# Stores taken one product later, ACT copies for the rotary swap, and token differences under the first head, in a diffusion layer kernel on one core

## The chip, the core and the metric

One program runs on one core of a Trainium2 chip. Five engines work side by side and wait for each other by semaphores: TensorE (PE in the profile, with its weight loads as PEld), VectorE (DVE), ScalarE (ACT), GpSimd (POOL) and SyncE (SP), whose queue here issues nearly all DMAs. Each engine takes its instructions strictly in the order in which the built program lists them, so an instruction that waits holds all that stand behind it. The metric is device microseconds for one execution.

## The reference

One layer over 1024 latent tokens and 256 context tokens, D = 1024, 4 retention heads and 4 mLSTM heads of width 128, then a SwiGLU feed-forward part of width 2816 and a last norm. Shortened:

```python
hx = modulate(rms_norm(x, norm1_gain), sh1, sc1)
rq, rk, rv, rg, mq, mk, mv, mo, mg, bg_ret, bg_ml = (hx @ w for w in split(w_in))
rq, rk = apply_rope(rq, cos, sin), apply_rope(rk, cos, sin)   # halves of each head: t1*cos - t2*sin, t2*cos + t1*sin
ret, ml = bidirectional_scans(...)                            # chunks of 128 tokens, both directions, context first
y_ret = head_norm(ret) * silu(rg)
y_ml = head_norm(sigmoid(mo) * ml)
merged = sigmoid(bg_ret) * (y_ret @ w_ret_up) + sigmoid(bg_ml) * (y_ml @ w_ml_up)
x = x + g1 * (merged @ w_out)
x = x + g2 * swiglu(modulate(rms_norm(x, norm2_gain), sh2, sc2), w_ffn_in, w_ffn_out)
return rms_norm(x, final_gain)
```

## The kernel before

**Products.** Activations stand with features on the partitions. Each float32 operand is split into a high and a low half (`split`: ACT makes the high half, DVE the low one), and a product is 12 matmuls of 128x128x512. The 16 input blocks of the 8 heads (for head `u`, part 0 is k and v, part 1 is q and the gate) and the 8 blocks of the branch gates `bg` are 256 output columns each. All but the first head's run as `winograd_block`: seven products in place of eight, over sums and differences of the four token quadrants (`t1` to `t4`, the token differences) and of the weight quadrants (`Factors`). Products 1, 3, 5 and 7 add up in one PSUM tile (`ch`), the others use two `ts` tiles; DVE or ACT takes the four results out (`put`, line 279) into `kt` tiles, and snapshots of the chain are ACT copies (line 284).

**The first head** is computed directly, since the differences aren't there yet: eight pieces of product for the first 512 tokens, four with `kh` 0 and four with `kh` 1 for the others, the gate product in between. Only then are the token differences built (lines 656 to 668): for each of four k tiles DVE and POOL form differences in `wt` tiles and `split` writes `t1` to `t4`.

**Side work.** `run_blocks` calls `tick` after each product. A tick does what `pending` holds (transposes of k and v to token layout, delayed by 2 or 4 ticks) and then advances generators: `gates` (the mLSTM gate rows, with running sums along 1280 tokens as DVE scans, lines 709 and 710), `scan(u)` (both directions of a head's scan: kv chunks loaded through a ring of six `kv` tiles, decayed on POOL at line 814, multiplied at line 828, added on DVE at line 833), and `ada2`. A scheduler turns the code into one list per engine, by its own guess of when each thing is ready.

**Rotary.** For retention heads `rotated` swaps the two partition halves of a result by two DMAs of 64x512 each (lines 562 and 563), POOL multiplies by sin (565), DVE by cos and adds (567, 568, or 570, 571 for q). The tables `cosT`, `sinT` are loaded once.

**Stores.** Each result is stored by a DMA that SP issues directly behind its producer in the code (lines 557, 579, 588, 590, 930, 991); SP waits in its queue until the result is there, and loads stand behind it.

**y_ret.** At the seventh `bg` block `load_y_ret` first drains all side work, then loads eight tiles of the retention output and splits them, all before that block's own work in the code; `load_split` and `Factors` share three `stg` tiles.

## Time and profile before

| | before |
|---|---|
| median of 3 runs | 1673.01 us (1670.24 to 1678.15) |
| the profiled execution | 1677.59 us, span 1675.8 us |
| PE busy | 1584.7 us, 95% of the span, 7478 matmuls |
| DVE, ACT, POOL busy | 1003.3 us (60%), 704.5 us (42%), 459.4 us (27%) |
| chain that ended last | PE 74%, DVE 8%, DMA 7%, POOL 4%, ACT 3% |
| DMA | 261.39 MB, mean 156 GB/s |

PE is the bound over the whole span, but the shares hide stages: from 1060 us on PE hardly pauses, and most of what it waits for lies in the first 770 us. So the stretches are read one by one, with what PE waited for in each.

### The profile page before, as it was taken

To read this page: it belongs to the slowest core of one execution; us is meant where nothing else is said; L and a number is where in the kernel's file an instruction comes from. 1 tells how busy PE (TensorE), PEld (TensorE's weight loads), DVE (VectorE), ACT (ScalarE), POOL (GpSimd) and SP (SyncE) were. 2 spreads that over 40 slices of the span, in tenths; PEclk is the share of its full clock that TensorE was granted. 3 is DMA by queue.
4 is the path that set the end of the run, shared out by engine and by line. 5 is a ranking of instruction groups with operands and counts; after the bars stand their busy time and mean duration, and the time that the engine had idled before them with its cause. 6 is when DMAs were issued, how large, how long until landed. Compare 5 with 4: busy or idle time off the path is not lost.

```text
span 1675.8 us, 22635 instructions
## 1 busy us (share of the span) xinstructions
PE 1584.7 (95%) x7478; PEld 1286.0 (77%) x7478; DVE 1003.3 (60%) x1835; ACT 704.5 (42%) x1370; POOL 459.4 (27%) x512
## 2 busy tenths in 40 slices
PE   7999889989999899988999999999999999999997
PEld 2677667777887778777888777888888888888887
DVE  4575896767667776655444667555555554636343
ACT  3653433444435466565223344344343334524230
POOL 0133424444344345420121225222222322001001
PEclk9999899999999999998999999999999999999998
DMA  8753337777668676544646332222222224835531
GB/s 286 261 157 112 92 92 236 225 221 229 216 205 254 209 217 199 183 134 155 200 145 218 114 95 83 82 89 82 95 82 88 84 81 145 272 105 169 182 96 51
DMA packets 186469, 261.39 MB, mean 156 GB/s; under 512 B 19264, under 2 KB 85952, under 8 KB 186352
## 3 DMA queue, kind: packets, MB, share of 16 engines
q1 hardware_dynamic: 184480, 257.85, 48.6%
q10 hardware_dynamic: 1872, 2.10, 0.4%
q8 instruction: 59, 0.97, 0.2%
q14 instruction: 58, 0.48, 0.1%
HBM read 199.30 MB, written 56.38 MB: 153 GB/s over the span
## 4 chain that ended last, share of the span: by engine, by line
PE 74%; DVE 8%; DMA 7%; POOL 4%; ACT 3%; issue 3%; SPq 1%; DVEq 0%; POOLq 0%; ACTq 0%
PE ch L249 22%; PE ts L249 18%; DMA kv<-kv_d 3%; PE ch L1257 2%; PE ch L1256 2%; PE ch L1255 2%; PE ts L1257 2%; PE ts L1255 2%; PE ts L1256 2%; PE sc L395 2%; DMA stg<-wada 1%; POOL hid L1125 1%; PE ts L104 1%; PE ch L104 1%; PE ts L103 1%
## 5 line engine op out<-in xcount | busy, mean ns | idle before, releaser
L183 DVE TENSOR_TENSOR fw<-raw,fw 128x512 fp32r<-128x512 f32 x305 | 225.8, 746 | 147.7 <-ACT fw L182 144.5
L249 PE MATMUL ts<-A,fw 128*128 128x512 f32 x1200 | 300.1, 397 | 2.1 <-DVE A L387 0.9
L182 ACT CAST fw<-raw 128x512 fp32r<-128x512 f32 x305 | 187.5, 620 | 257.7 <-PE ch L1257 84.5
L249 PE MATMUL ch<-A,fw 128*128 128x512 f32 x1176 | 291.6, 396 | 0.0
L249 PE MATMUL ch<-t,fw 128*128 128x512 f32 x1008 | 257.3, 401 | 6.7 <-ACT u L284 3.6
L249 PEld LDWEIGHTS ts<-A,fw 128*128 128x128 f32 x1200 | 224.6, 190 | 50.4 <-DVE A L387 3.0
L249 PEld LDWEIGHTS ch<-A,fw 128*128 128x128 f32 x1176 | 219.3, 189 | 46.4 <-issue 1.0
L249 PEld LDWEIGHTS ch<-t,fw 128*128 128x128 f32 x1008 | 189.1, 192 | 46.6 <-ACT u L284 4.2
L249 PE MATMUL ts<-t,fw 128*128 128x512 f32 x504 | 133.7, 410 | 24.6 <-ACT fw L182 8.4
L1125 POOL TENSOR_TENSOR hid<-hid,sg 128x512 f32<-128x512 f32 x44 | 90.2, 2062 | 214.7 <-DVE hid L279 198.1
L249 PEld LDWEIGHTS ts<-t,fw 128*128 128x128 f32 x504 | 96.5, 196 | 46.9 <-ACT fw L182 8.8
L221 POOL TENSOR_TENSOR stg<-raw,raw 128x512 f32<-128x512 f32 x42 | 62.7, 1494 | 225.9 <-DVE fw L183 95.1
L284 ACT COPY u<-ch 128x512 f32<-128x512 f32 x104 | 60.8, 585 | 142.0 <-PE ch L249 136.2
L183 DVE TENSOR_TENSOR fw<-stg,fw 128x512 fp32r<-128x512 f32 x126 | 97.2, 771 | 30.9 <-ACT fw L182 30.8
L182 ACT CAST fw<-stg 128x512 fp32r<-128x512 f32 x126 | 78.3, 623 | 70.8 <-DVE stg L221 41.0
L814 POOL TENSOR_SCALAR vs<-kv,dcol 128x128 f32<-128x128 f32 x72 | 57.8, 808 | 58.8 <-DMA kv<-kv_d 34.6
L1247 POOL TENSOR_SCALAR cp<-cp,cpack 128x256 f32<-128x256 f32 (+1 forms) x6 | 8.2, 1361 | 222.2 <-ACT stg L1301 222.2
L828 PE MATMUL sc<-vs,kv 128*128 128x128 f32 (+1 forms) x288 | 52.1, 284 | 16.1 <-POOL vs L814 12.4
L814 POOL TENSOR_SCALAR vs<-kv,colq 128x129 f32<-128x129 f32 x72 | 51.9, 726 | 45.7 <-DMA kv<-kv_d 21.9
L828 PEld LDWEIGHTS sc<-vs,kv 128*128 128x128 f32 x288 | 44.8, 192 | 23.8 <-POOL vs L814 14.9
L183 DVE TENSOR_TENSOR fw<-s,fw 128x512 fp32r<-128x512 f32 x42 | 30.7, 732 | 43.5 <-ACT fw L182 43.4
L959 DVE SCALAR_TENSOR_TENSOR acc<-stg,silu_c,acc 128x512 f32<-128x512 f32 x56 | 43.9, 784 | 17.6 <-DMA stg<-wada 17.1
(363 smaller groups left out, 2918.4 us busy)
## 6 DMA issues: line engine op xcount, KB each, us to landing
raw<-wffn SPq DMA_DIRECT2D x88, 256.0 KB
raw<-wfo SPq DMA_DIRECT2D x88, 256.0 KB
kv<-kv_d SPq DMA_DIRECT2D x152, 128.0 KB
raw<-win SPq DMA_DIRECT2D x64, 256.0 KB
stg<-wada SPq DMA_DIRECT2D x64, 256.0 KB
hid_d<-hid SPq DMA_DIRECT2D x44, 256.0 KB
hraw<-hid_d SPq DMA_DIRECT2D x40, 256.0 KB
araw<-wada SPq DMA_DIRECT2D x32, 256.0 KB
```

The lines of the kernel that those rows point to most:

```text
L182: nc.scalar.copy(hi, x)
L183: nc.vector.tensor_tensor(out=lo, in0=x, in1=hi.bitcast(F32), op=ALU.subtract)
L221: eng.tensor_tensor(out=o, in0=x, in1=y, op=op)
L249: nc.tensor.matmul(ps, lhsT=w[wp_][:, c], rhs=x[xp][k], start=start and k == i == 0, stop=cont or (stop and k == 3 and i == 2), skip_group ...
L284: nc.scalar.copy(o, chain)
L814: nc.gpsimd.tensor_scalar(out=vs, in0=kv[d, n][1], scalar1=col, scalar2=None, op0=ALU.mult)
L828: nc.tensor.matmul(ps, lhsT=kv[d, n][0], rhs=vsd.pop((d, n)), start=True, stop=True)
L959: nc.vector.scalar_tensor_tensor(out=acc, in0=raw, scalar=s, in1=acc, op0=ALU.mult, op1=ALU.add)
L1125: nc.gpsimd.tensor_tensor(out=c, in0=c, in1=sgs[f, hf], op=ALU.mult)
L1255: nc.tensor.matmul(ps, lhsT=w[0][:, c], rhs=h[0][:, t], start=kt == 0, stop=False)
L1256: nc.tensor.matmul(ps, lhsT=w[0][:, c], rhs=h[1][:, t], start=False, stop=False)
L1257: nc.tensor.matmul(ps, lhsT=w[1][:, c], rhs=h[0][:, t], start=False, stop=kt == 2 * NG - 1)
```

## The change

Six edits. (1) Every store, gate store and y store is put into `pending` by `later(1, store, ...)` or `later(2, ...)`, so that SP gets it one or two ticks after its producer. (2) `rotate` runs one tick after its result and swaps the halves by two ACT copies; it loads its 512 columns of cos and sin each time (256 KB each, from the ring of two `rp` tiles). (3) The token differences are built inside the first head: `first_factor` behind each of the four `kh` 0 pieces, `other_factors` behind the gate product. (4) Two 36x1280 subtractions of `gates` go from DVE to POOL. (5) The `kv` ring has 8 tiles, `wt` 5; y results use `wt` and the `bg` results `kt`. (6) `load_y_ret` is a generator beside the last two `bg` blocks, a tile per tick, loaded three ticks ahead of its split, through `wt`.

```diff
-        return pw.tile([P, 512], dt, tag="wt", bufs=4, name=nm("wt"))
+        return pw.tile([P, 512], dt, tag="wt", bufs=5, name=nm("wt"))
...
+    def store(dst, src):
+        nc.sync.dma_start(dst, src)
...
-        nc.sync.dma_start(dst, o.rearrange("p (n c) -> p n c", n=4))
+        later(1, store, dst, o.rearrange("p (n c) -> p n c", n=4))
+
+    def rotate(c, hf, scale):
+        cs, sn = (pw.tile([P, 512], F32, tag="rp", bufs=2, name=nm("rp")) for _ in range(2))
+        for t, key in ((cs, "cosT"), (sn, "sinT")):
+            nc.sync.dma_start(t, a[key][:, hf * 512:hf * 512 + 512])
+        sw = wt()
+        nc.scalar.copy(sw[0:64], c[64:P])
+        nc.scalar.copy(sw[64:P], c[0:64])
+        nc.gpsimd.tensor_tensor(out=sw, in0=sw, in1=sn, op=ALU.mult)
...
-            sw = wt()
-            nc.sync.dma_start(sw[0:64], c[64:P])
-            nc.sync.dma_start(sw[64:P], c[0:64])
...
+            if f == 0:
+                if ret:
+                    later(1, rotate, c, hf, QSCALE if part else None)
+                elif part:
+                    nc.scalar.activation(c, c, AF.Copy, scale=QSCALE)
+                later(2 if ret else 1, store, qk_d[u][:, 1 - part, t], c)
+                if part == 0:
+                    later(4 if ret else 2, transpose_out, c, kv_d[u][:, n0, 0, :])
...
-                if kh == 1:
+                if kh == 0:
+                    first_factor(2 * key + f)
+                else:
...
             gate_products(CTX + 512, 512, lambda i, kt: xh[1][i][:, kt, :])
+            for k in range(4):
+                other_factors(k)
...
-        nc.vector.tensor_tensor(out=gi, in0=gi, in1=bb, op=ALU.subtract)
-        nc.vector.tensor_tensor(out=bb, in0=bb, in1=m, op=ALU.subtract)
+        nc.gpsimd.tensor_tensor(out=gi, in0=gi, in1=bb, op=ALU.subtract)
+        nc.gpsimd.tensor_tensor(out=bb, in0=bb, in1=m, op=ALU.subtract)
...
-            t = bt([P, 2 * P + 1], "kv", 6)
+            t = bt([P, 2 * P + 1], "kv", 8)
...
-            nc.sync.dma_start(y_d[u, j0 // 4], sy)
+            later(1, store, y_d[u, j0 // 4], sy)
...
                 if blk == 6:
-                    load_y_ret()
+                    drain()
+                    es_b.close()
+                    beside(load_y_ret())
...
+        raws_ = []
+        for i in range(11):
+            if i < 8:
+                raws_.append(wt())
+                nc.sync.dma_start(raws_[i], y_d[i % 4, i // 4])
+            if i >= 3:
+                hf, k = (i - 3) // 4, (i - 3) % 4
                 y_ret[hf].append(tuple(py_.tile([P, 512], F32R, name=nm("yr")) for _ in range(2)))
-                load_split(y_d[k, hf], *y_ret[hf][k])
+                split(*y_ret[hf][k], raws_[i - 3])
+            yield
```

The matmuls of PE are the same in number and kind. What moves is the order on the engines that feed it, at three places.

ACT, end of the first head, before: `e` is the gate product's result, `kt` the first head's four results for the second 512 tokens (line 641), `fw` weight halves, `t` and `A` the halves of the token differences (`wt` their inputs).

```order
L615 COPY e_1305<-sc_1288 128x512
L641 COPY kt_1320<-ts_1228 128x512
L182 CAST fw_1505<-stg_1503 128x512
L641 COPY kt_1341<-ch_1249 128x512
L182 CAST fw_1533<-stg_1531 128x512
L641 COPY kt_1355<-ts_1262 128x512
L182 CAST fw_1536<-raw_1483 128x512
L641 COPY kt_1384<-ch_1275 128x512
L556 COPY wt_1381<-sc_1376 128x512
L182 CAST t_1390<-wt_1388 128x512
```

The same place of the change (the `kt` copies are line 668 now; lines 564 and 565 are the new swap copies):

```order
L616 COPY e_1333<-sc_1316 128x512
L182 CAST t_1373<-wt_1369 128x512
L182 CAST A_118<-wt_1370 128x512
L182 CAST t_1394<-wt_1384 128x512
L668 COPY kt_1412<-ts_1229 128x512
L182 CAST fw_1514<-stg_1512 128x512
L182 CAST t_1389<-wt_1385 128x512
L182 CAST A_118<-wt_1386 128x512
L564 COPY wt_1430<-kt_1412 64x512
L565 COPY wt_1430<-kt_1412 64x512
L668 COPY kt_1436<-ch_1258 128x512
```

Before, no half of a token difference stood ahead of the four `kt` copies; now the halves of the third and fourth k tile, which wait for POOL's differences, stand ahead of the first and the second of them.

DVE in `gates`, behind the last running sum (4x1024), before: `gi`, `bb` and the others are `g` tiles, line 279 takes a product's result out of a `ts` tile, lines 719 and 720 are the two subtractions.

```order
L710 SCALAR_TENSOR_TENSOR g_1575<-g_1576,g_1575,g_1574 4x1024
L570 SCALAR_TENSOR_TENSOR kt_1910<-kt_1910,rp_977 128x512
L713 COPY gm_1581<-g_1575 4x9
L714 COPY gm_1581<-g_1575 4x1
L571 SCALAR_TENSOR_TENSOR kt_1910<-wt_1912,kt_1910 128x512
L715 COPY gm_1581<-g_1575 4x1
L716 COPY gm_1581<-g_1575 4x7
L719 TENSOR_TENSOR g_1574<-g_1574,g_1578 36x1280
L279 TENSOR_TENSOR kt_1999<-ts_1986,u_1892 128x512
L720 TENSOR_TENSOR g_1578<-g_1578,g_1575 36x1280
L183 TENSOR_TENSOR fw_2039<-raw_1951,fw_2039 128x512
L721 TENSOR_TENSOR g_1576<-g_1578,gm_1581 36x1280
```

And in the change, where line 727 is the former 721:

```order
L716 SCALAR_TENSOR_TENSOR g_1587<-g_1588,g_1587,g_1586 4x1024
L719 COPY gm_1593<-g_1587 4x9
L720 COPY gm_1593<-g_1587 4x1
L721 COPY gm_1593<-g_1587 4x1
L722 COPY gm_1593<-g_1587 4x7
L279 TENSOR_TENSOR kt_2027<-ts_2014,u_1916 128x512
L183 TENSOR_TENSOR fw_2081<-s_2079,fw_2081 128x512
L183 TENSOR_TENSOR fw_2084<-raw_1985,fw_2084 128x512
L568 TENSOR_TENSOR kt_2027<-kt_2027,rp_2029 128x512
L727 TENSOR_TENSOR g_1588<-g_1590,gm_1593 36x1280
L569 TENSOR_TENSOR kt_2027<-kt_2027,wt_2033 128x512
L735 COPY gm_1595<-g_1590 4x10 x2
```

The first line 279 moves ahead of the subtractions, and line 727, which reads what POOL now makes, still stands ahead of the next line 279.

DVE at `load_y_ret`, before: `yr` are the low halves of the retention output, `fw` from `stg`, `s` and `raw` those of the running block's weights.

```order
L183 TENSOR_TENSOR yr_8014<-stg_8015,yr_8013 128x512
L183 TENSOR_TENSOR yr_8020<-stg_8021,yr_8019 128x512
L183 TENSOR_TENSOR yr_8026<-stg_8027,yr_8025 128x512
L183 TENSOR_TENSOR yr_8032<-stg_8033,yr_8031 128x512
L221 TENSOR_TENSOR stg_8052<-raw_7861,raw_7863 128x512
L183 TENSOR_TENSOR yr_8038<-stg_8039,yr_8037 128x512
L221 TENSOR_TENSOR s_8057<-stg_8052,raw_7859 128x512
L183 TENSOR_TENSOR fw_8054<-stg_8052,fw_8054 128x512
```

And in the change:

```order
L183 TENSOR_TENSOR fw_8071<-raw_7925,fw_8071 128x512
L131 TENSOR_TENSOR rst_7992<-rs_7991 128x8
L132 SCALAR_TENSOR_TENSOR rst_7992<-rst_7992,var_7989 128x8
L133 SCALAR_TENSOR_TENSOR rs_7991<-rst_7992,rs_7991 128x8
L923 TENSOR_TENSOR o_7639<-o_7639,rs_7991 128x512
L923 TENSOR_TENSOR o_7856<-o_7856,rs_7991 128x512
L183 TENSOR_TENSOR fw_8076<-stg_8074,fw_8076 128x512
L221 TENSOR_TENSOR stg_8240<-raw_8145,raw_8147 128x512
L279 TENSOR_TENSOR kt_8044<-ts_7927,wt_8042 128x512
L221 TENSOR_TENSOR s_8245<-stg_8240,raw_8143 128x512
L183 TENSOR_TENSOR fw_8137<-stg_8135,fw_8137 128x512
L183 TENSOR_TENSOR yr_8167<-wt_8097,yr_8166 128x512
```

Before, seven of the eight `yr` halves stood ahead of the running block's second weight factor (`fw_8054`); now its factors stand ahead of the first `yr` half.

## Rows read from the trace of the kernel before

**Rows 1.** Windows by stretch: start:end length, busy us (instructions) per engine, clock, DMA, GB/s.
```profile
102.00:156.20 54.20, 54.20 (x251) 44.51 (x249) 32.75 (x55) 18.69 (x32) 18.55 (x15) 1.00 0.37 114
156.20:192.30 36.10, 25.28 (x91) 17.95 (x90) 30.12 (x35) 15.54 (x27) 20.00 (x18) 0.86 0.25 72
...
218.00:246.00 28.00, 20.58 (x91) 15.86 (x90) 27.62 (x31) 9.35 (x13) 4.78 (x2) 0.88 0.24 68
246.00:742.00 496.00, 464.56 (x2535) 390.18 (x2535) 340.41 (x781) 246.50 (x586) 212.94 (x339) 0.99 0.67 210
742.00:770.00 28.00, 18.60 (x69) 14.31 (x68) 17.30 (x25) 13.43 (x24) 2.95 (x2) 0.76 0.55 171
```

**Rows 2.** Timeline of PE at the y loads: start, us, line, what [idle before <-releaser].
```profile
757.99 1.22 PE L249 MATMUL ts<-t,fw 128*128 128x512 f32 x2 [8.38 <-ACT fw L182]
...
767.70 2.88 PE L249 MATMUL ts<-A,fw 128*128 128x512 f32 x12
770.42 2.88 PE L249 MATMUL ch<-t,fw 128*128 128x512 f32 x12
```

**Rows 3.** Timeline of POOL: first and last of eight token-difference instructions.
```profile
164.71 1.28 POOL L663 TENSOR_TENSOR wt<-t,t 128x512 f32<-128x512 f32 x1
...
184.68 1.59 POOL L666 TENSOR_TENSOR wt<-t,wt 128x512 f32<-128x512 f32 x1 [0.80 <-DVE wt L664]
```

**Rows 4.** Timeline of PE beside the running sums of the gates.
```profile
227.13 0.61 PE L249 MATMUL ch<-A,fw 128*128 128x512 f32 x2
235.16 1.22 PE L249 MATMUL ts<-t,fw 128*128 128x512 f32 x2 [7.42 <-DVE kt L279]
236.18 5.36 PE L249 MATMUL ch<-A,fw 128*128 128x512 f32 x15
```

**Rows 5.** Timeline of DVE there: first and last running sum, two results taken out.
```profile
218.81 2.81 DVE L709 TENSOR_TENSOR_SCAN g<-g,g 4x1280 f32<-4x1280 f32 x1
...
228.78 2.31 DVE L710 TENSOR_TENSOR_SCAN g<-g,g,g 4x1024 f32<-4x1024 f32 x1
...
234.44 0.67 DVE L279 TENSOR_TENSOR kt<-ts,u 128x512 f32<-128x512 f32 x1
...
240.40 0.69 DVE L279 TENSOR_TENSOR kt<-ts,wt 128x512 f32<-128x512 f32 x1
```

**Rows 6.** Waits of PE, 236 to 745: us in total, times, longest us.
```profile
PE sc L828 <- POOL vs L814: 12.4, 8, 3.2
...
PE sc L828 <- POOL kv L803: 2.3, 1, 2.3
```

**Rows 7.** Pieces of the chain that ended last: start us, us, what.
```profile
155.42 4.09 DMA wt<-kt
...
275.18 0.07 SPq L588
...
275.82 3.76 DMA kv<-kv_d
...
398.76 5.37 DMA kv<-kv_d
```

**Rows 8.** Groups by line and form, 102 to 260: count | busy us, mean ns | idle.
```profile
L666 POOL TENSOR_TENSOR wt<-t,wt 128x512 f32<-128x512 f32 x4 | 7.2, 1805 | 8.2 <-issue 4.9 <-DVE wt L664 3.3
...
L663 POOL TENSOR_TENSOR wt<-t,t 128x512 f32<-128x512 f32 x4 | 5.1, 1273 | 0.0
...
L183 DVE TENSOR_TENSOR t<-wt,t 128x512 fp32r<-128x512 f32 x12 | 12.1, 1036 | 4.3 <-POOL wt L666 3.5 <-ACT t L182 0.9
...
L719 DVE TENSOR_TENSOR g<-g,g 36x1280 f32<-36x1280 f32 x1 | 1.5, 1483 | 0.0
```

**Rows 9.** Timelines of ACT, DVE and PE: a 128x512 copy; a rotated k and its transposes.
```profile
129.87 0.59 ACT L556 COPY wt<-sc 128x512 f32<-128x512 f32 x1
...
251.76 0.69 DVE L568 TENSOR_TENSOR kt<-kt,wt 128x512 f32<-128x512 f32 x1
...
254.47 0.60 PE L554 MATMUL sc<-cpack,kt 128*128 128x128 f32 x4
```

More of the change, by code (lines that the diff above doesn't have):

```diff
@@ L518, in body @@
     plain_pair(w_qg, a["win"][1], 1, last=tuple(st.tile([P, 512], F32R, tag="ss", bufs=2, name=nm("wl")) for _ in range(2)))
-    rot = [pw.tile([P, S], F32, tag="rp", bufs=2, name=nm("rp")) for _ in range(2)]
-    for t, key in zip(rot, ("cosT", "sinT")):
-        nc.sync.dma_start(t, a[key])
-    cosT, sinT = rot
     gw = st.tile([P, KT, 16], F32, name="gw")
@@ L538, in body, with later, run_pending @@
     pending = []
-    def store_tokens(c, dst, ticks):
-        pending.append([ticks, lambda: transpose_out(c, dst)])
-    def run_pending(all_=False):
+    def later(ticks, fn, *args):
+        pending.append([ticks, fn, args])
+    def run_pending():
         for p in list(pending):
             p[0] -= 1
-            if p[0] <= 0 or all_:
+            if p[0] <= 0:
                 pending.remove(p)
-                p[1]()
+                p[1](*p[2])
+    def store(dst, src):
+        nc.sync.dma_start(dst, src)
     def transpose_out(c, dst):
@@ L630, in body, with put_factor, first_factor, other_factors @@
             scaled_x(1, 4 * (w is w_qg) + 2 * f + 1)
+    b_all = quad(xh[0], 0), quad(xh[0], 4), quad(xh[1], 0), quad(xh[1], 4)
+    t4 = b_all[2]
+    t1, t2, t3 = (tuple([] for _ in range(2)) for _ in range(3))
+    def put_factor(t, d, *where):
+        for s in range(2):
+            t[s].append(t_tile(*where[s]))
+        split(t[0][-1], t[1][-1], d)
+    def first_factor(k):
+        d = wt()
+        nc.vector.tensor_tensor(out=d, in0=x_raw[1][k], in1=x_raw[0][k], op=ALU.subtract)
+        put_factor(t1, d, (2, 0, k), (2, 1, k))
+    def other_factors(k):
+        x11, x21, x12, x22 = x_raw[0][k], x_raw[0][4 + k], x_raw[1][k], x_raw[1][4 + k]
+        d3, d2, d4 = wt(), wt(), wt()
+        nc.gpsimd.tensor_tensor(out=d3, in0=x22, in1=x12, op=ALU.subtract)
+        nc.vector.tensor_tensor(out=d2, in0=d3, in1=x11, op=ALU.add)
+        put_factor(t2, d2, (1, 0, k), (3, 0, k))
+        nc.gpsimd.tensor_tensor(out=d4, in0=x21, in1=d2, op=ALU.subtract)
+        put_factor(t3, d3, (3, 1, k), (1, 1, k))
+        split(t4[0][k], t4[1][k], d4)
     ps4 = {}
@@ L644, in body @@
             gate_products(CTX + 512, 512, lambda i, kt: xh[1][i][:, kt, :])
+            for k in range(4):
+                other_factors(k)
     es_st.close()
-    b_all = quad(xh[0], 0), quad(xh[0], 4), quad(xh[1], 0), quad(xh[1], 4)
-    t4 = b_all[2]
-    t1, t2, t3 = (tuple([] for _ in range(2)) for _ in range(3))
-    def put_factor(t, d, *where):
-        for s in range(2):
-            t[s].append(t_tile(*where[s]))
-        split(t[0][-1], t[1][-1], d)
-    for k in range(4):
-        d = wt()
-        nc.vector.tensor_tensor(out=d, in0=x_raw[1][k], in1=x_raw[0][k], op=ALU.subtract)
-        put_factor(t1, d, (2, 0, k), (2, 1, k))
-    for k in range(4):
-        x11, x21, x12, x22 = x_raw[0][k], x_raw[0][4 + k], x_raw[1][k], x_raw[1][4 + k]
-        d3, d2, d4 = wt(), wt(), wt()
-        nc.gpsimd.tensor_tensor(out=d3, in0=x22, in1=x12, op=ALU.subtract)
-        nc.vector.tensor_tensor(out=d2, in0=d3, in1=x11, op=ALU.add)
-        put_factor(t2, d2, (1, 0, k), (3, 0, k))
-        nc.gpsimd.tensor_tensor(out=d4, in0=x21, in1=d2, op=ALU.subtract)
-        put_factor(t3, d3, (3, 1, k), (1, 1, k))
-        split(t4[0][k], t4[1][k], d4)
     t_all = (t1, t2, t3, t4)
@@ L923, in put_y @@
                 nc.tensor.transpose(py[:, i * P:(i + 1) * P], ot[j0 // 4][:, i, :], ident)
-            sy = stage()
+            sy = wt()
             if ret:
@@ L983, in drain @@
     def drain():
-        while side:
+        while pending or side:
             tick()
@@ L990, in done @@
             nc.scalar.activation(c, c, AF.Sigmoid)
-            nc.sync.dma_start(bg_d[blk, f, hf], c)
+            later(1, store, bg_d[blk, f, hf], c)
         return done
```

42 lines of the change are left out of this document (13 added, 29 removed).

## The prediction

> **What bounds the kernel now.** I read the page first: PE is busy for 95% of the span, and the change leaves its matmuls alone. So the change can only take away, or add, time in which PE pauses or runs slowly. I then cut the first 770 us into stretches and read the windows of each [rows 1]. The first column after the length is PE's busy time with its count; the number after the five engines is the mean granted clock, where 1.00 is 2.4 GHz throughout and 0.50 would be 1.2 GHz, its other level.
>
> To know what a stretch should cost I need PE's undisturbed pace. Two products of 12 matmuls that follow each other without a pause start at 767.70 and 770.42 [rows 2]: 2.72 us a product, 0.227 us a matmul. (The durations overlap, so starts are the thing to use.) The loss of a stretch is its length less its matmuls at that pace. It holds two things: PE's idle time, and matmuls that run longer where the granted clock is below 1.00, which here is only seen where PE also paused [rows 1].
>
> - First head, 102.0 to 156.2: PE is busy for all of it, while DVE works 32.75 and ACT 18.69 of 54.20 us. No loss; room on the other engines.
> - Token differences, 156.2 to 192.3: 36.1 us less 91 x 0.227 (20.6) is a loss of **15.5 us**, 10.8 of it idle, the rest at a mean clock of 0.86.
> - Gates, 218 to 246: between 227.13 and the end of the run of 15 matmuls at about 241.4, 19 matmuls take 14.2 us in place of 4.3 [rows 4], a loss of **9.9 us**. One pause carries it: 7.42 us for a result that DVE takes out at 234.44.
> - Scans, 246 to 742: 496 less 464.6 busy is 31.4 us idle, in many small pieces; the clock is 0.99.
> - y loads, 742 to 770: 28 less 69 x 0.227 (15.7) is **12.3 us**, at a clock of 0.76, behind a wait of 8.38 us for ACT's weight half [rows 2].
>
> **The change part by part.** The sum is made against the profiled execution, 1677.6 us.
>
> *Token differences.* Their eight POOL instructions run from 164.71 to 186.27, 21.6 us in all [rows 3]. Four of 1.27 and four of 1.81 us are 12.3 us of POOL's own work [rows 8], the rest is waiting for DVE and for tiles. In the change they stand inside the first head, under PE's 54 us. The inputs of the last two k tiles need `wt` tiles, which the late stores give back later, so I place the start at 133 to 139 (an estimate: about six tenths into the head) and the end 21.6 us later (no faster, since its steps stay in line), at 155 to 161. PE's next products start at about 156, so most of the loss goes. Not all: in the new order on ACT the halves of the third and fourth k tile stand ahead of the first head's last `kt` copies, and a PSUM tile is only free when its copy is done. That is a wait of between 0 (all done by 156) and 8 us (POOL ends at 161, then DVE's half at 1.04 and two ACT steps of 0.6 [rows 8, 9], and slow matmuls behind the pause); I take 4. Gain **11.5**, from 7.5 to 15.5.
>
> *Gates.* Before, the last running sum ends at 228.78 + 2.31 = 231.1, and then two products' results must pass DVE, at 234.44 and 240.40 [rows 5]; two subtractions of 1.48 us stand ahead of them [rows 8]. In the change the first result goes ahead of what is left of the subtractions, 2 x 1.48 = 3.0 us earlier. But line 727 still stands ahead of the second and now waits for POOL. POOL's subtraction has no row; 128x512 takes it 1.27 us [rows 8], so 1280 columns are about 3.2 us each, 6.4 for two. Line 727 then starts at about 231.1 + 6.4 and ends 1.5 later, at T = 239, and the second result is out by 239.7, against 241.1 before. So the pause is split in two more than it is shortened. The sums may also start later: they need gate rows that come back through memory, and the new table loads stand on SP's queue around them. I take **0**, between -3.4 and +9.9 (all of the loss).
>
> Here the bound of -3.4 comes from the rows: POOL takes 6.4 us for what cost DVE 3.0, and if DVE cannot work meanwhile, that difference is lost. The rows do show interference: `t<-wt` on DVE takes 1.04 us a piece beside POOL's work, against 0.69 for a like sized instruction [rows 8, 9], and POOL's line 666 1.81 against 1.27 for line 663 [rows 8]. The Trainium skill, "SBUF — State Buffer", section "Who interferes with whom", speaks against this edit: a DVE instruction with two SBUF inputs and a GpSimd instruction that reads SBUF share a port pair, and whoever comes first keeps it for its whole instruction. By that rule DVE's work with two SBUF inputs would stop for up to 6.4 us and this term would be -3.4, for 1644 us in the end; the trace agrees in direction, as the rows just named show, though half slower is less than fully blocked.
>
> *Stores and the `kv` ring.* The chain of waits shows the pattern: at 275.18 SP is held by the store of line 588, and the load of `kv` behind it then takes 3.76 us; at 398.76 such a load takes 5.37 us [rows 7]. PE feels this as waits for POOL's `vs` (12.4 us in 8 waits) and for `kv` itself (2.3) [rows 6]: 14.7 of the 31.4 us. A store that comes a tick (2.72 us) later no longer holds the queue, and two more `kv` tiles let loads start earlier. POOL's own work on `vs` and DVE's state additions stay, so I take **9** of the 14.7. Bounds: 18 (all of it and some 3 us of slow matmuls after the pauses) and -5 (nothing gained, and results held one tick longer in the rings of `kt` and `wt`, two waits of 2.72).
>
> *Rotary.* A swap DMA is 4.09 us [rows 7]; two ACT copies of 64x512, at no more than the 0.59 of a 128x512 copy [rows 9], are 1.2. The rotation begins one tick later, 2.72 us, so POOL's multiplication starts at 2.72 + 1.2 = 3.9 against 4.1, and the transposes of the finished k, four ticks behind, keep their slack of 2.0 us (252.45 to 254.47 [rows 9]). The tables now come 16 times as two loads of 256 KB. That is 8 MB for 5 MB of swaps and resident tables, beside a DMA share of 0.24 to 0.67 [rows 1]; with two tiles a rotation's tables can load as soon as the one before it is done. **0** while they land ahead; a late one is a rival below.
>
> *y loads.* The new order puts the running block's factors ahead of the `yr` halves, which is just what PE waited for at 757.99. Gain **11**, from 8 (a short wait stays) to 12.3.
>
> *The fifth `wt` tile, the results of gates and y in other rings:* their copies are the same in number, in ACT's 54 us with 18.69 busy or the like [rows 1]. 0.
>
> Sum: 11.5 + 0 + 9 + 0 + 11 = 31.5, so 1677.6 - 31.5 = 1646.1 in an execution like the profiled one. That one lies 4.6 us above the median of the runs, so the median after is about **1641 us**.
>
> **The rivals.** A difference under 0.5%, 8.4 us, is about what a measurement here cannot tell from none; so faster means below 1664.6 and slower above 1681.4.
>
> - *Less: the waits move on.* The token differences leave their 8 us, the scans give nothing since DVE is next in line, and the gates lose 3.4. 7.5 + 0 - 3.4 + 11 = 15: **1658 us**. For it: DVE is busy for 27.62 of 28 us in the gates [rows 1]. Against: the waits for `kv` and `vs` are real waits for loads.
> - *More.* All terms at their upper bounds: 15.5 + 9.9 + 18 + 12.3 = 55.7, **1617 us**; some of it, 1622.
> - *The tables come late for k.* A table load that is only issued when the swap is, and takes 5.37 us as the slow `kv` load, is 5.37 - 2.0 = 3.4 us over the slack of the transposes, and PE stands in line for it; with 1.9 us of slow matmuls behind such a pause (at the gates 15 matmuls took 5.2 in place of 3.4) that is 5.3 us. At the six k rotations of heads 1 to 3 it is 32 us, and the gain is gone: **1673 us**, no change. For it: SP waits in its queue, and loads for a tile still in use now stand there. Against: a block of seven products has two rotations, so they come 3.5 x 2.72 = 9.5 us apart, and the tables of the next can land in between.
> - *Slower.* The same wait, but at all twelve rotations of these heads, since `kv` and weight loads stand behind a table load that SP holds for a tile of the rotation before: 12 x 5.3 = 64 less 31.5: **1705 us**. It decides from (31.5 + 8.4) / 12 = 3.3 us per rotation. Against: the 9.5 us between rotations are more than the 3.9 us to POOL's start and the three instructions behind it, so the wait should be short.
>
> **How the numbers follow.** The forecast (gain of 23 to 45) 0.53, less 0.22, more 0.06, tables late and no change 0.11, slower 0.08. Faster is the sum of the first three, 0.81. The range leaves out about half of "more" at its lower end, and the slower and most of the unchanged case at the upper, some 2 in 10: 1622 to 1665 us; the forecast's own range is 1628 to 1650.
>
> **What would show it.** Right: PE busy for over 29 of the 36 us behind the first head; no wait of PE of more than 2 us in the seventh and eighth `bg` block; PE's waits for `vs` and `kv` below 6 us; in the gates still a pause of 3 to 7 us and POOL instructions of 36x1280 of about 3.2 us. Wrong: PE's transposes of line 554 waiting for rotated k, `rp` loads standing in the chain of waits, weight loads late behind them, or a first head in which PE now pauses since DVE and ACT are full.

## The result, and the profile after

The changed kernel takes 1662.51 us (median of 8 runs, 1656.5 to 1665.72) against 1674.56 (8 runs): a ratio of 0.9926, with a 95% interval from 0.9904 to 0.9948. The medians differ by 12.1 us, where 32 were forecast. The time lies in the range, but the likeliest case did not come: it was the first rival, "the waits move on". Its sum of 15 us was made against the profiled execution, and the profiled spans differ by 1675.8 - 1660.5 = 15.3 (the execution profiled before lies 3.0 us above its median, the one after on its median). Its parts, 7.5, 0, -3.4 and 11, are near the 7.9, -0.1, -6.1 and 13.0 of the table below, but the nothing of the scans turns out to be a gain and a loss of about the same size.

Since PE's work is the same, the two traces can be laid over each other by ACT's snapshots `u<-ch` and `wt<-ch` (line 284), which come in the same order in both. The table has the start of five of them, in us, and how much earlier or later the same snapshot is after the change; the last column says which stretch lies between it and the one above.

| snapshot | before | after | difference | the stretch that ends here, and its share |
|---|---|---|---|---|
| 5th | 202.17 | 193.25 | -8.9 | start (-1.0 by 93 us) and token differences: -7.9 |
| 11th | 254.67 | 251.91 | -2.8 | gates: +6.1 |
| 61st | 744.21 | 741.52 | -2.7 | scans: +0.1 |
| 62nd | 767.90 | 752.21 | -15.7 | y loads: -13.0 |
| 126th | 1410.70 | 1395.14 | -15.6 | the rest: nothing |

The windows of the changed kernel say the same; columns as in [rows 1], and these are the places of its second, fourth, fifth and sixth row.

```profile
155.20:183.60 28.40, 22.93 (x96) 18.94 (x97) 19.20 (x24) 15.14 (x27) 14.40 (x14) 0.88 0.47 116
...
209.20:243.50 34.30, 21.73 (x92) 16.85 (x90) 33.80 (x32) 10.19 (x15) 11.27 (x6) 0.80 0.27 83
243.50:739.30 495.80, 466.15 (x2535) 391.18 (x2535) 341.48 (x785) 263.52 (x609) 221.88 (x340) 0.99 0.69 213
739.30:754.50 15.20, 15.20 (x67) 12.34 (x67) 10.72 (x16) 9.63 (x18) 0.49 (x1) 1.00 0.78 256
```

At the y loads PE is now busy throughout, at the full clock (2.4 GHz). In the gates DVE is busy for 33.8 of 34.3 us, and PE loses 34.3 - 92 x 0.227 = 13.4 us, where the same sum over the window before was 28.0 - 91 x 0.227 = 7.3. (Both windows hold small matmuls too, which take less than 0.227 us, so these sums come out lower than the 9.9 of the prediction.) The scans' idle time is 29.65 us, against 31.4.

What PE waited for over the whole run, the largest but the first loads: us, times, longest.

```profile
PE ch L249 <- ACT wt L284: 10.3, 1, 10.3
...
PE sc L929 <- DVE o L923: 8.4, 7, 1.6
PE sc L554 <- ACT kt L668: 5.8, 1, 5.8
PE sc L834 <- POOL vs L820: 5.5, 4, 2.3
```

The first is the gates, the third the end of the first head. Lines 834 and 820 are 828 and 814 of before, 929 and 923 are 923 and 917. So the wait that I priced in the scans did shrink: 12.4 us for `vs` [rows 6] became 5.5, and the 2.3 for `kv` is gone. But the wait for the normed output `o` at the end of each head grew, from 4.6 to 8.4, and other small waits for DVE with it.

**The gates in the trace after.** Timelines of PE, DVE, ACT and POOL; line 716 is the running sum, 722 a tiny copy, 725 and 726 the moved subtractions, 564 and 565 the swap copies.

```profile
218.43 2.88 PE L249 MATMUL ch<-A,fw 128*128 128x512 f32 x12
231.61 4.12 PE L249 MATMUL ch<-A,fw 128*128 128x512 f32 x11 [10.30 <-ACT wt L284]
...
238.00 1.09 PE L554 MATMUL sc<-cpack,kt 128*128 128x128 f32 x4 [2.27 <-DVE kt L279]
...
223.64 2.31 DVE L716 TENSOR_TENSOR_SCAN g<-g,g,g 4x1024 f32<-4x1024 f32 x1
...
226.29 2.65 DVE L722 COPY gm<-g 4x7 f32<-4x7 f32 x1
228.97 0.69 DVE L279 TENSOR_TENSOR kt<-ts,u 128x512 f32<-128x512 f32 x1
229.58 4.08 DVE L183 TENSOR_TENSOR fw<-s,fw 128x512 fp32r<-128x512 f32 x1
...
234.79 1.47 DVE L727 TENSOR_TENSOR g<-g,gm 36x1280 f32<-36x1280 f32 x1
...
237.16 0.69 DVE L279 TENSOR_TENSOR kt<-ts,wt 128x512 f32<-128x512 f32 x1
...
225.99 1.27 ACT L729 ACTIVATE g<-g 36x1280 f32<-36x1280 f32 x1 [9.41 <-DVE g L716]
229.70 0.62 ACT L564 COPY wt<-kt 64x512 f32<-64x512 f32 x1 [2.44 <-DVE kt L279]
230.33 0.62 ACT L565 COPY wt<-kt 64x512 f32<-64x512 f32 x1
230.97 0.58 ACT L284 COPY wt<-ch 128x512 f32<-128x512 f32 x1
...
226.03 2.88 POOL L725 TENSOR_TENSOR g<-g,g 36x1280 f32<-36x1280 f32 x1 [14.18 <-DVE g L716]
228.99 2.88 POOL L726 TENSOR_TENSOR g<-g,g 36x1280 f32<-36x1280 f32 x1
231.84 1.28 POOL L566 TENSOR_TENSOR wt<-wt,rp 128x512 f32<-128x512 f32 x1
```

Read it from PE upward. PE waits for ACT's snapshot at 230.97; ACT has it behind the two swap copies; these wait for DVE's line 279 at 228.97; and that stands behind a copy of 4x7 elements that takes 2.65 us. The copy ends at 228.94, as POOL's first subtraction ends at 228.91. Line 183, behind line 279, takes 4.08 us in place of 0.68 and spans POOL's second subtraction and its multiplication behind that. Line 279 itself, whose input `ts` is in PSUM, takes its usual 0.69 us beside POOL.

**Behind the first head.** ACT's timeline: the first two `kt` results (line 668) with what stands between them, and PE's wait.

```profile
154.57 0.58 ACT L668 COPY kt<-ts 128x512 f32<-128x512 f32 x1
...
156.40 0.62 ACT L182 CAST t<-wt 128x512 fp32r<-128x512 f32 x1 [0.73 <-DVE wt L650]
158.12 0.62 ACT L182 CAST A<-wt 128x512 fp32r<-128x512 f32 x1 [1.11 <-POOL wt L652]
158.77 0.62 ACT L564 COPY wt<-kt 64x512 f32<-64x512 f32 x1
...
160.04 0.58 ACT L668 COPY kt<-ch 128x512 f32<-128x512 f32 x1
...
160.68 1.12 PE L554 MATMUL sc<-cpack,kt 128*128 128x128 f32 x4 [5.79 <-ACT kt L668]
```

### The profile page after: what moved, and what is told of

Same layout as the page of the kernel before. It is cut to its first block, busy times and chain, and to the rows that moved or that the text cites. A ratio compares the mean times of both kernels' runs of the same rounds, so it can differ in the third digit from the quotient of the medians.

```text
span 1660.5 us, 22679 instructions
## 1 busy us (share of the span) xinstructions
PE 1580.3 (95%) x7478; PEld 1286.2 (77%) x7478; DVE 1004.8 (61%) x1833; ACT 729.3 (44%) x1406; POOL 473.0 (28%) x514
## 4 chain that ended last, share of the span: by engine, by line
PE 66%; DVE 8%; DMA 4%; POOL 3%; issue 2%; ACT 2%; SPq 1%; DVEq 0%; POOLq 0%; ACTq 0%
PE ch L249 21%; PE ts L249 17%; PE ch L1269 2%; PE ch L1270 2%; PE ch L1268 2%; PE ts L1268 2%; PE ts L1270 2%; PE ts L1269 2%; POOL hid L1138 1%; PE ts L104 1%; DVE fw L183 1%; PE ch L104 1%; PE ts L102 1%; PE ts L103 1%; PE ch L102 1%
## 5 line engine op out<-in xcount | busy, mean ns | idle before, releaser
L183 DVE TENSOR_TENSOR fw<-raw,fw 128x512 fp32r<-128x512 f32 x305 | 222.4, 736 | 146.4 <-ACT fw L182 146.0
L249 PE MATMUL ch<-A,fw 128*128 128x512 f32 x1176 | 293.7, 397 | 10.3 <-ACT wt L284 10.3
L249 PE MATMUL ch<-t,fw 128*128 128x512 f32 x1008 | 253.1, 398 | 3.4 <-ACT u L284 3.4
L249 PE MATMUL ts<-t,fw 128*128 128x512 f32 x504 | 127.2, 400 | 0.0
L183 DVE TENSOR_TENSOR fw<-stg,fw 128x512 fp32r<-128x512 f32 x126 | 93.8, 745 | 37.8 <-ACT fw L182 37.5
L183 DVE TENSOR_TENSOR fw<-s,fw 128x512 fp32r<-128x512 f32 x42 | 34.5, 822 | 49.4 <-ACT fw L182 49.4
L221 DVE TENSOR_TENSOR stg<-raw,raw 128x512 f32<-128x512 f32 x42 | 43.7, 1040 | 22.9 <-DMA raw<-wffn 16.6
L965 DVE SCALAR_TENSOR_TENSOR acc<-stg,silu_c,acc 128x512 f32<-128x512 f32 x56 | 47.4, 846 | 15.5 <-DMA stg<-wada 15.3
```

What stands on the lines that cost most here:

```text
L183: nc.vector.tensor_tensor(out=lo, in0=x, in1=hi.bitcast(F32), op=ALU.subtract)
L221: eng.tensor_tensor(out=o, in0=x, in1=y, op=op)
L249: nc.tensor.matmul(ps, lhsT=w[wp_][:, c], rhs=x[xp][k], start=start and k == i == 0, stop=cont or (stop and k == 3 and i == 2), skip_group ...
L965: nc.vector.scalar_tensor_tensor(out=acc, in0=raw, scalar=s, in1=acc, op0=ALU.mult, op1=ALU.add)
```

## The experiments

All ratios are to the kernel before on the same chip; 0.001 is 1.7 us. Where a stretch is named, it is read from the same five snapshots, as their difference to the kernel before. Each kernel was traced once, and the runs come from several chips, on which the kernel before has medians from 1674.56 to 1680.3 us. None of the edits is aimed at the stretch from the 62nd to the 126th snapshot, and still its share comes out between -3.4 and +3.1 us over the runs; so a share of 3 us in a long stretch cannot be told from none. The short stretch of the gates repeats better.

**1. Subtractions back on DVE** (a_subs)

```diff
-        nc.gpsimd.tensor_tensor(out=gi, in0=gi, in1=bb, op=ALU.subtract)
-        nc.gpsimd.tensor_tensor(out=bb, in0=bb, in1=m, op=ALU.subtract)
+        nc.vector.tensor_tensor(out=gi, in0=gi, in1=bb, op=ALU.subtract)
+        nc.vector.tensor_tensor(out=bb, in0=bb, in1=m, op=ALU.subtract)
```

> The changed kernel with edit 4 undone: the two 36x1280 subtractions of the gates are back on DVE. Beside POOL's two, DVE's 4x7 copy took 2.65 us in place of 0.15 and its line 183 4.08 in place of 0.68. Theory 1 (DVE stands still while POOL holds the port): both go back to their short times, the second result of DVE line 279 comes about 4 us earlier, PE's second pause there (2.27 us) goes and the first (10.3 us) stays at 9 to 11; the whole takes 2 to 4 us less, 1659 to 1660.5 us. Theory 2 (the pause comes from what stands ahead on ACT and from the running sums alone): the two 1.48 us subtractions cost DVE what the others cost POOL, no difference, 1662 to 1663 us.

0.9871 (0.9846 to 0.9895). PE's and DVE's timelines there:

```profile
228.00 1.65 PE L249 MATMUL ts<-t,fw 128*128 128x512 f32 x3 [7.30 <-DVE kt L279]
...
225.69 0.15 DVE L722 COPY gm<-g 4x7 f32<-4x7 f32 x1
225.86 1.48 DVE L725 TENSOR_TENSOR g<-g,g 36x1280 f32<-36x1280 f32 x1
227.27 0.68 DVE L279 TENSOR_TENSOR kt<-ts,u 128x512 f32<-128x512 f32 x1
```

Theory 1, and more than I gave it: the copy is back at 0.15 us, both pauses shrink (10.3 to 7.3, 2.27 to nothing), and the eleventh snapshot is 9.2 us early in place of 2.8. The whole loss of the changed kernel in the gates is this one edit: their share is between +5.0 and +6.8 us in all nine traces with the subtractions on POOL, and +0.2, +1.0 and +0.5 in runs 1, 9 and 14, which have them on DVE in the old order. Of the 6.4 us the scans take 3.2 back by the snapshots (61st: -5.9), but PE is idle there for only 1.5 us more (31.2 in place of 29.7), and by the ratios the run gains 9.2 us; so it is not shown that the scans take anything back.

**2. The swap by DMA** (a_swap)

```diff
-        nc.scalar.copy(sw[0:64], c[64:P])
-        nc.scalar.copy(sw[64:P], c[0:64])
+        nc.sync.dma_start(sw[0:64], c[64:P])
+        nc.sync.dma_start(sw[64:P], c[0:64])
```

> The changed kernel with only the swap of edit 2 undone: the two 64x512 copies are DMAs again, the tables are still loaded each time. Theory 1 (in the gates, and at the end of the first head, the two copies stand on ACT ahead of the snapshot or the result that PE waits for, and wait for DVE): PE's first pause in the gates falls from 10.3 to about 7 us and its pause behind the first head from 5.8 to about 4.5; 4 to 6 us less in these two stretches, and the scans (246 to 742 us before) as they are, 1657 to 1659 us. Theory 2 (the copies take load off SP's queue and what they cost on ACT is hidden): loads behind the swaps come late again, 1664 to 1670 us.

0.9972 (0.9954 to 0.999), slower by 7.7 us than the changed kernel's ratio. Theory 2. The gates did not gain (eleventh -2.1): without the copies ahead of the snapshot PE's pause is 9.96 us there, now for a weight half that DVE's line 183 makes, 2.73 us beside POOL. The scans lost 11.6 us. With the tables loaded anew beside them, the swaps belong off SP's queue.

**3. Stores at once** (a_now)

```diff
-            later(1, store, y_d[u, j0 // 4], sy)
+            store(y_d[u, j0 // 4], sy)
...
             nc.vector.scalar_tensor_tensor(out=c, in0=sw, scalar=scale, in1=c, op0=ALU.mult, op1=ALU.add)
+        store(dst, c)
```

The stores of transposes, gate and branch gate results likewise; the last line is the end of `rotate`.

> The changed kernel with edit 1 undone: every store is issued directly behind its producer, that of a rotated tile directly behind the rotation. Theory 1 (as predicted: stores that wait at the head of SP's queue make kv loads late, and taking that away is worth what PE waited for them): PE's waits for POOL's decayed kv go back from 5.5 to 10 or more, and the time goes up by 6 to 10 us, 1668 to 1672 us. Theory 2 (in the scans PE waits for DVE's part of the side work as soon as kv is on time, so the late stores are worth nothing in the end): within 3 us of 1662.5, with the waits shifted from DVE back to POOL.

0.9919 (0.9896 to 0.9943): no difference. PE's wait for `vs` is 5.7 us, with the changed kernel's 5.5, and POOL's waits for `kv` loads between 246 and 742 us are 14.5 us, against 7.1. Theory 2 holds for the time, though not its reason: the `kv` loads are nearly as punctual without the late stores, so these were not what made them so. In the one trace the scans lose 5.2 us, with PE idle for 34.7 in place of 29.7; the times do not bear that out, but the interval leaves room for some 3 us that the late stores are worth.

**4. y loads in one burst** (a_yburst)

```diff
-                    drain()
-                    es_b.close()
-                    beside(load_y_ret())
+                    load_y_ret()
```

`load_y_ret` is that of the kernel before.

> The changed kernel with edit 6 undone: the eight y loads and their splits all stand ahead of the seventh branch gate block, through the stg ring, as before. Theory 1 (the whole gain of 13 us between 742 and 768 us is that order): 13 us more, 1675 us, with a wait of PE of some 8 us for a weight half. Theory 2 (half of it was the loads' own queue, which the late stores have emptied): 5 to 8 us more, 1668 to 1670 us.

0.9929 (0.9908 to 0.9951), no measurable difference; in the trace 4.4 us of the end are lost, 3.6 of it at the y loads, where a wait of 1.85 us for ACT's `fw` is left of the 8.38 [rows 2]. Below both expectations. So the generator is not the only thing that took the 13 us away.

**5. Running sums spread** (a_gates), **6. with the last differences written later** (a_best)

```diff
         nc.gpsimd.memset(rm[32:36, P - 1::P], 0.0)
         yield
+        yield
...
-                    beside(gates(), 0.4)
+                    beside(gates(), 1.0)
...
-            for k in range(4):
+            for k in range(2):
                 other_factors(k)
...
+                    if key == 0:
+                        other_factors(2 + f)
```

There are 14 such yields, and one more behind each running sum; the subtractions are on DVE. The lower two pieces of the diff, of which the last stands behind the pieces with `kh` 1, are in a_best alone.

> The changed kernel with the two subtractions back on DVE and the gates' running sums spread: the generator yields after each of the six sums, starts them 14 ticks later and runs at 1.0 in place of 0.4 steps a tick, so that DVE takes products' results out between two sums. Theory 1 (PE's first pause of 7 to 10 us in the gates is nothing but DVE's 11 us of sums in one piece): no pause of PE over 2 us there, 8 to 10 us gained in that stretch against the kernel with the subtractions on DVE alone; with a part lost again in the scans, a ratio to the kernel before of 0.981 to 0.985. Theory 2 (the pause comes from the exponentials and copies behind the sums): a pause of 4 us or more stays, ratio 0.986 to 0.988.

> As the run with spread sums, and the token differences of the third and fourth k tile are written behind the first and second piece of the first head's second half, so that ACT's first copy stands ahead of one more pair of halves. Theory 1 (PE's pause of 5.8 us behind the first head is ACT's order): the pause falls to 2 to 4 us, 2 to 3 us more gained, ratio 0.979 to 0.984. Theory 2 (it is POOL's and DVE's chain of differences, which ends when it ends): the pause moves to the first products that read the last differences and the time stays within 1 us of the run with spread sums.

0.9878 (0.9854 to 0.9903) and 0.9885 (0.9862 to 0.9908). Neither beats run 1. A pause of 9.59 us for line 279 is still there in a_gates, and the gates' share is +4.0, where it was +0.2 in run 1: the sums stand apart, but DVE is busy for 37.17 of 38 us, from 209.2 to 247.2. Theory 1 fell; theory 2 has the pause and the ratio right, but the pause is still for a result behind a sum. That DVE's amount of work bounds this stretch, whatever its order, is argued from its busy time, not tested. In a_best the pause behind the first head fell to 4.3 us and the fifth snapshot came 1.1 us earlier, less than the 2 to 3 of theory 1, and nothing of it is left in the end.

**7. y results in stg** (a_ystg)

```diff
-            sy = wt()
+            sy = stage()
```

> The changed kernel with one part of edit 5 undone: the heads' y results go through the three stg tiles again, which the weight factors use too, while the y loads stay a generator. With the loads in one burst only 4 of the 13 us came back, so 9 belong to something else. Theory 1 (they belong to the y stores, which keep stg tiles from the weight factors): 5 to 10 us lost up to the end of the y loads, ratio 0.996 to 0.999. Theory 2 (either of the two repairs is enough alone, the loss before needed the burst and the held tiles together): at most 3 us lost, ratio 0.992 to 0.994.

0.9857 (0.9831 to 0.9882): faster by 0.7%, where both theories had no change or a loss. The stretch that gains is none that I had expected: the scans, -6.6 us between the eleventh snapshot (-2.6) and the 61st (-9.2), with PE idle for 23.2 us in place of 29.7. Runs 9 and 14, which have this edit too, gain 7.3 and 4.9 there. That is a good part of the forecast gain of the scans, which had been missing. Runs 10, 11 and 13 ask why.

**8. Tables resident, rings as before** (a_tab)

```diff
+    rot = [pw.tile([P, S], F32, tag="rp", bufs=2, name=nm("rp")) for _ in range(2)]
...
-            t = bt([P, 2 * P + 1], "kv", 8)
+            t = bt([P, 2 * P + 1], "kv", 6)
```

The `wt` ring has four tiles again, and `rotate` reads its half of the two tables.

> The changed kernel with the tables of the rotation loaded once (1 MB, resident) and the rings that pay for it as before: six kv tiles, four wt tiles. The ACT copies stay. Theory 1 (the 16 double loads of tables wait in SP's queue for a free tile and hold kv and weight loads there, and the longer rings bring less than that costs): 3 to 7 us less up to 742 us, ratio 0.988 to 0.991. Theory 2 (the longer kv ring is what made kv come on time): PE's waits for decayed kv go up from 5.5 to 10 or more and the time by 4 to 8 us, ratio 0.995 to 0.998. No difference if both are small, 0.991 to 0.994.

0.9935 (0.991 to 0.9959): the middle case by the time. In the scans 4.2 us are lost by the snapshots (PE idle for 31.9 us in place of 29.7), and POOL's wait for `kv` loads goes from 7.1 to 34.5 us; but PE's wait for `vs` is 4.5 us, no longer than with eight tiles, so theory 2 has no support there. The reloaded tables cost no more than the longer rings bring.

**9. Both repairs** (a_two): edits 1 and 7 together.

> The changed kernel with two pieces undone together: the gates' subtractions on DVE and the y results in the stg ring. Each alone gave some 6 us, the one in the gates, the other in the scans. Theory 1 (two causes in two stretches): they add, 11 to 14 us less than the changed kernel, ratio to the kernel before 0.979 to 0.983. Theory 2 (the scans give back part of what comes in earlier, as with the spread sums): 7 to 10 us less, ratio 0.984 to 0.987.

0.9844 (0.9819 to 0.9869), which is 13.7 us below the changed kernel by the ratios; the profiled span is 1646.1, 14.4 us below the changed kernel's. The two ways in which I had stated the theories do not agree: 13.7 us is theory 1, the ratio is theory 2. By the snapshots the two gains add up, 5.2 us in the gates and 7.4 in the scans, as theory 1 has it.

**10. Two stg tiles** (a_stg2): `bufs=3` of `stg` becomes `bufs=2`.

> The changed kernel with two stg tiles in place of three, y results in wt tiles. In the scans DVE waits 26.5 us for ACT's weight halves, 10.6 before and 8.8 with y results in stg. Theory 1 (with stg tiles always free the weight factors are prepared so early that ACT and DVE stand in line for PE to free a weight half, and the scans' work stands behind them): fewer stg tiles hold the factors back as the y stores did, DVE's wait for ACT's halves falls below 15 us and the scans take 3 to 7 us less; outside them the tight ring may cost as much. Theory 2 (the y results in wt tiles are late themselves, or keep wt tiles from others): DVE's wait and the scans stay as in the changed kernel within 2 us, or get longer.

0.9946 (0.9926 to 0.9965). DVE's wait for ACT's halves stays at 26.2 us, and the scans get 6.0 us longer: theory 1 in that form fell. A smaller ring does not keep the factors back in the way that the y results did.

**11. y in stg, six kv tiles** (a_ykv6): run 7's edit, and `"kv", 8` becomes `"kv", 6`.

> The kernel with the y results in stg, with six kv tiles in place of eight. Theory 1 (as predicted, the longer ring is part of what makes kv come on time): POOL's waits for kv loads go up from 20.8 us, PE's for decayed kv from 5.2 us to 8 or more, and the time by 3 to 6 us, ratio 0.989 to 0.992. Theory 2 (the rotating halves no longer standing in SP's queue are enough): within 2 us of the kernel with eight, ratio 0.985 to 0.987.

0.9927 (0.9903 to 0.9951). POOL's waits in the scans, in the kernel before:

```profile
POOL vs L814 <- DMA kv<-kv_d: 56.5, 40, 4.2
```

In the kernel of run 7:

```profile
POOL vs L820 <- DMA kv<-kv_d: 20.8, 11, 5.2
```

And with the shorter ring:

```profile
POOL vs L820 <- DMA kv<-kv_d: 63.4, 36, 4.9
```

Theory 1: PE waits 13.6 us for `vs` in place of 5.2, and the scans lose 8.4 us (their share goes from -6.6 to +1.8). Beside the reloaded tables the ring of eight is what makes `kv` punctual; with the late stores but six tiles all of it is gone. With the tables resident, six tiles left PE's wait for `vs` at 4.5 us (run 8, though with the y results in `wt`), so a part of the lateness may be the table loads' own; six tiles and resident tables were not tried with y in stg.

**12. Edit 6 alone** (b_ygen): the kernel before with the generator of the y loads.

> The kernel before with edit 6 alone: the y loads are a generator beside the last two branch gate blocks and use the four wt tiles, while y results stay in stg and gate results in wt. Theory 1 (the order at that place is the whole of that loss, whatever came before it): 11 to 14 us less, ratio 0.991 to 0.994, all of it between 742 and 770 us. Theory 2 (the wt ring, shared with the gate results and their stores, takes the place of stg): 3 to 8 us less, ratio 0.995 to 0.998.

0.9937 (0.9916 to 0.9958), theory 1: -11.3 us between the 61st snapshot (+2.2) and the 62nd (-9.1).

**13. A turn in the ring** (a_ytouch), **14. both repairs and later differences** (a_two_tok: run 9 with the differences of run 6)

```diff
+            mark = stage()
+            nc.scalar.copy(mark[:, 0:1], sy[:, 0:1])
             later(1, store, y_d[u, j0 // 4], sy)
```

> The changed kernel with the y results in wt tiles as they are, and behind each of them a copy of one column into a stg tile that nobody reads: the y results take their turn in the stg ring again without using it. Theory 1 (the turn in the ring decides: it keeps the next weight factors behind the head's norm in DVE's and ACT's order): DVE's wait for ACT's weight halves in the scans falls from 26.5 us to below 13, PE's wait for the norm from 8.4 to about 5, and the scans take 5 to 9 us less; ratio 0.985 to 0.989. Theory 2 (the y results in wt tiles keep these from transposes, swaps and snapshots): as the changed kernel, ratio 0.991 to 0.994.

> The kernel with the gates' subtractions on DVE and the y results in stg, and with the token differences of the third and fourth k tile written behind the first and second piece of the first head's second half. Theory 1 (PE's pause of 5.8 us behind the first head is in good part ACT's order): the pause falls to about 4.3 us, as in the run with spread sums, and the whole by 1 to 3 us, ratio 0.982 to 0.984. Theory 2 (the scans take it back): no difference, 0.984 to 0.986.

a_ytouch: 0.989 (0.9856 to 0.9924), median 1657.45 us. The interval allows the changed kernel's 0.9926, so the time alone does not decide; the trace does for a part. DVE's wait for ACT's weight halves between 246 and 742 us (us, times, longest) in the changed kernel:

```profile
DVE fw L183 <- ACT fw L182: 26.5, 24, 3.3
```

With y results in stg (run 7):

```profile
DVE fw L183 <- ACT fw L182: 8.8, 11, 2.5
```

With y results in `wt` and the turn in the ring (run 13):

```profile
DVE fw L183 <- ACT fw L182: 12.1, 15, 2.5
```

PE's wait for the norm is 5.0 us with the turn, in place of 8.4 (5.3 with y in stg). The 25th snapshot (388 us) is 4.7 us early, as with y in stg (5.3; the changed kernel 1.5). At 466 us 3.3 us are lost in one place, where PE waits 2.19 us for the scan's state `sf` (line 839), with y in stg 0.41. In the end the scans gain 2.5 in place of 6.6, less than the 5 to 9 of theory 1.

What the turn changes stands in DVE's timeline at the first scan's end. Line 919 opens the head's norm and 923 ends it, 183 and 221 are weight factors of the next block. In the changed kernel, with a line each of POOL and PE below:

```profile
311.37 0.75 DVE L965 SCALAR_TENSOR_TENSOR acc<-stg,silu_c,acc 128x512 f32<-128x512 f32 x1 [0.57 <-DMA stg<-wada]
312.04 0.68 DVE L183 TENSOR_TENSOR fw<-stg,fw 128x512 fp32r<-128x512 f32 x1
312.64 1.26 DVE L919 TENSOR_SCALAR var<-ssq 128x8 f32<-128x8 f32 x1
...
314.66 0.68 DVE L221 TENSOR_TENSOR s<-stg,raw 128x512 f32<-128x512 f32 x1
...
317.42 1.29 DVE L923 TENSOR_TENSOR o<-o,rs 128x512 f32<-128x512 f32 x2
...
312.20 1.67 POOL L221 TENSOR_TENSOR stg<-raw,raw 128x512 f32<-128x512 f32 x1 [6.59 <-DVE acc L965]
...
318.26 0.63 PE L929 MATMUL sc<-cpack,o 128*128 128x128 f32 x4 [1.23 <-DVE o L923]
```

With y results in stg, whose order here is also that of the run with the turn:

```profile
312.40 0.17 DVE L919 TENSOR_SCALAR var<-ssq 128x8 f32<-128x8 f32 x1 [0.69 <-ACT junk L915]
...
314.88 1.29 DVE L923 TENSOR_TENSOR o<-o,rs 128x512 f32<-128x512 f32 x2
```

The norm's last step starts 2.5 us earlier where the factors take their turn behind the y results; PE stands at 317 us for just this `o`. Line 919 itself takes 1.26 us in the changed kernel, in place of 0.17, and ends at 313.90, as POOL's weight factor ends at 313.87. The same can be counted for all eight heads: from the start of line 919 to that of 923 there are 33.1 us in sum in the changed kernel, 21.1 before, 21.1 with y in stg and 21.3 with the turn. So the turn alone gives the norm back whole.

a_two_tok: 0.9813 (0.9783 to 0.9843), 1645.19 us (6 runs, 1643.83 to 1648.77), the fastest of all: 1.1% below the changed kernel by the ratios. The pause behind the first head is 4.2 us, as theory 1 said; the ratio is a little below its range, but the interval overlaps with run 9's, so what the later differences bring in time is not shown.

## Why the prediction was wrong, step by step

*What bounds the kernel.* Right. All of the difference in the table arises before 770 us, and nearly all of it where PE paused. Of the signs that I named, three came: PE is busy for 30.6 of the 36.1 us behind the first head, its waits for `vs` and `kv` sum to 5.5 us, and it has no wait over 2 us in the last two `bg` blocks. The fourth did not: the pause in the gates is 10.3 us, where 3 to 7 were named.

*Token differences, 11.5 forecast, 7.9 measured.* The mechanism was right: ACT's order leaves a pause of 5.79 us, and the first matmuls behind it are slow (12 take 5.2 us). Together that leaves 7.6 of the 15.5 us, near the upper end of 0 to 8, where I took 4; so the size of this term was off. POOL ends at 156.51 + 1.58 = 158.1, in the middle of 155 to 161.

*Gates, 0 forecast, 6.1 lost.* This is the first step that failed: the price of the moved subtractions. I had 6.4 us on POOL (it was 5.8) as a wait of line 727 alone, with the second result out 8.6 us after the last running sum (231.1 to 239.7), and a bound of -3.4 for "DVE cannot work meanwhile". That result was out 11.9 us after the sum (225.95 to 237.85), since DVE did stand still: its copy and its line 183 together took 5.9 us longer than they do alone, and line 727 started 2.9 us after POOL was done. What I left out is who is queued behind DVE; here it was ACT's swap copies, which edit 2 had just put ahead of the snapshot. They are the path and not the cause, since without them (run 2) PE waits as long for line 183 and the gates lose 6.8 us. So the first pause grew by 3.0 against run 1, and a second of 2.3 opened behind line 727, with slow matmuls after each. Run 1 shows the whole of it as that edit's. I also misread the old order: of the two subtractions only line 719 stood ahead of the first result, so its gain was 1.5 us and not 3.0. Here the Trainium skill, "SBUF — State Buffer", section "Who interferes with whom", was right against the milder reading that I took from [rows 8]: whoever comes first blocks the other for the whole instruction. The trace agrees: the copy ends 0.03 us after POOL's first subtraction.

*Stores and the kv ring, 9 forecast, 0 measured.* Two mistakes that hid each other. The wait that I priced went as forecast, 9.2 of the 14.7 us, but not by the stores: six tiles take 8.4 us of the gain away (run 11), and stores at once cost nothing measurable (run 3), so the late store at the head of SP's queue [rows 7] was a wait, but not the one that counted. The second step that failed is the line on edit 5 that I closed with "0". It cost about 6.6 us, which run 7 gets back: the y results left the stg ring, the next weight factors no longer took turns with them, and stood in the middle of the head's norm on DVE, 33.1 us for eight norms in place of 21.1. That PE's next wait would be for DVE's norm was in the first rival in general ("DVE is next in line"), without its cause.

*Rotary, 0 forecast.* Each copy took 0.62 us, a little more than the 0.59 that I had as the most. The copies alone are worth 7.7 us beside the reloaded tables (run 2); the room for the longer rings is that of the resident tables. No rotation was late by the 3.4 us of the third and fourth rival: PE's waits for a rotated tile (line 569) sum to 0.2 us in the whole trace. Both fell.

*y loads, 11 forecast, 13.0 measured.* Right; edit 6 alone gives 11.3. That the burst costs only 3.6 once the rest is changed shows that the loss needed two things at once. Run 4 has both the late y stores and their tiles out of stg, and which of the two eases the burst was not tried by itself.

*The sum.* 31.5 less 3.6 (differences), 6.1 (gates) and 9.1 (scans), and 2.0 more (y loads), is 14.7, and 1.0 came at the start: 15.7 us, the -15.6 of the table. The medians show 12.1, as the execution profiled before lies 3.0 us above its median; to which stretch these 3.0 belong is not known.

*Still open.* The turn in the ring brings back the norm, but 2.5 of 6.6 us in the scans by the trace; 3.3 of the other 4.1 are lost at the one wait for `sf`, and whether that is the y tiles' hold on `wt` or a different fall of the order was not settled. Nor was it settled whether the scans really take back 3 us in run 1.

## What to carry to other kernels

A ring of tiles is also an order: who takes a turn in it stands ahead or behind in the lists of all engines, so moving one user to another ring can cost as much as a wait that it frees, and a copy of one column into the ring helps to show whether it does. Before work goes from DVE to POOL, price it as POOL's time on DVE too, as long as DVE's next instructions are of the kinds that were held here, and then look at what is queued behind DVE's next result. Read a change by stretches with the same landmarks in both traces; the two spans alone would have shown 15 us gained, and not 21.9 gained and 6.1 given back, with a gain and a loss of some 7 us each hidden in the scans.

## What was not expected of the hardware

A DVE copy of 4x7 elements, from SBUF to SBUF, took 2.65 us beside a POOL subtraction and 0.15 without; a 128x512 subtraction 4.08 against 0.68. The eight traces with this order all show it, with 2.65 to 2.66 and 4.08 to 4.10 us. Both instructions end just behind one of POOL's (228.94 behind 228.91, and 233.66 behind 233.12), so this reads as a wait until POOL lets go, and not as a share of the speed.

Not every DVE instruction is held. Beside the same subtractions two copies of 4x1 took 0.14 and 0.13 us, and line 279, which has one input in PSUM, 0.69.

How many of POOL's instructions DVE waits for depends on the case. Line 183 waited through two in a row (to 231.87 and 233.12). In run 2, where another instruction of DVE comes first, DVE gets in behind each of POOL's, and then POOL's next one is the longer, 1.71 us for line 566 in place of 1.28 (DVE's lines first, then POOL's):

```profile
225.16 3.08 DVE L571 SCALAR_TENSOR_TENSOR kt<-kt,rp 128x512 f32<-128x512 f32 x1
228.27 1.11 DVE L722 COPY gm<-g 4x7 f32<-4x7 f32 x1
...
224.80 2.89 POOL L725 TENSOR_TENSOR g<-g,g 36x1280 f32<-36x1280 f32 x1 [13.14 <-DVE g L716]
227.64 1.71 POOL L566 TENSOR_TENSOR wt<-wt,rp 128x512 f32<-128x512 f32 x1
```

What decides between the two was not tried.
